# Input-projection weights requested on ScalarE's queue and a step later, stores of unit outputs a step later, next input rows a step sooner

## The chip, the cores and the metric

The program runs on one core of a Trainium2 chip. The metric is device time in microseconds (us) from one launch, shorter is better. Names used below: PE is TensorE (matmuls; PEld is its weight load), DVE is VectorE, ACT is ScalarE, POOL is GpSimd, SP is SyncE, which computes nothing and in this kernel only issues transfers (DMAs). ACT can issue DMAs too, between its own instructions and in their order.

## The reference

One encoder layer over two sequences (1024 and 2048 tokens of 1024 channels, all float32). The normed input goes through one wide projection; an FNet (Fourier) group and a bidirectional state-space group (24 heads of 64, in chunks of 128 tokens) work on its columns; both are gated, joined and projected back, then a gated per-layer embedding is added and a final norm taken.

```python
u = rms_norm(h, norm_w)
proj = u @ w_in
z_f, u_f, z_s, xbc, dt_raw = split(proj)
y_f = fft2(u_f).real @ w_fmix * silu(z_f)
xbc = silu(conv5(xbc) + conv_b)                 # -> xs, Bm, Cm
y_s = ssd(xs, dt_f, A_f, Bm, Cm) + flip(ssd(flip(...))) + D * xs
y_s = group_norm(y_s * silu(z_s)) * ssd_norm_w
h = h + concat(y_f, y_s) @ w_out
h = h + (p @ w_ple_in) * sigmoid(h @ w_ple_gate)
y = rms_norm(h, final_norm_w)
```

## The kernel before

Three phases follow each other: projection with the state-space group (to about 2085 us), the Fourier group (to about 2230 us), and the output projections with the end of the layer. The change touches the first alone. Its tokens come in three blocks of 1024: P (the short sequence), S1 and S2 (the halves of the long one).

**Steps.** In a block, 41 jobs each make 128 columns of the projection. A job has three pieces, one to a third of the block's tokens; a piece is 24 matmuls on a split of the float32 operands (`wh`, `wl` the weights' high and low part, `uh`, `ul` the tokens'), into one of three PSUM buffers `ps`. One piece is one step of a schedule that is written out by hand: `pre(s, f)` and `post(s, f)` put a function ahead of or behind the piece of step `s`, and every engine gets its instructions in that order. A block has 123 pieces. A state-space unit `u` (two heads; twelve to a block, one started every nine steps for most) is spread over some twenty steps by `Unit.plan`.

**Weights.** `Job.load` asks for the weights. In block P they come raw (`wr`, 512 KB); `Job.split` scales them on ACT (L327), makes `wh` (L333) there and `wl` on POOL (L334), and both are stored to memory (`WPd`). In S1 and S2 `load` fetches the stored `wh` and `wl` (512 KB each, L308), and `split` rounds them on ACT (L323). There are three buffers for `wh` and three for `wl`, so that a load waits for the last reader of the buffer that it takes.

**A unit's transfers.** `rows_in` asks for rows `R` (two of 256 KB at each of four steps, L551), which POOL cuts two steps later (`affine_select`, L559); ACT takes the exponent a step after that (L569), DVE joins them, PE uses them (`pd`, L586). POOL also makes `xw` (L598), which PE needs for the states (`pst`, L618). `decays` fetches `er` (eight requests of 64 partitions for a unit, L646). `gated` multiplies on POOL (L669; in S1 L674 too), and `out` stores `y` (L678) and, in S1, `zT` (L680).

**Next rows.** At a block's end `x_in` fetches nine tiles `xt` of the next block's tokens (L124), `x_norm` scales them on ACT (L225), and `x_turn` transposes them on PE (L239) into `uh` and `ul`.

**Queues.** Before the change all transfers of this phase are issued by SP, in order: an entry that has to wait holds all behind it. A finished transfer is told by one of eight semaphores (`DMAHW0` to `DMAHW7` in the listings of order), which are dealt out in turn over all transfers of the program; a transfer waits for the one that had its semaphore before to land. That is so for every issuing engine.

Of the kernel before, what the change touches and what calls it, by code (L numbers as in the profile page):

```python
# [9 lines left out]
F32 = mybir.dt.float32  # L10
# [8 lines left out]
P = 128  # L19
# [37 lines left out]
def tile_hybrid_encoder(ctx: ExitStack, tc: tile.TileContext, a):  # L57
    nc = tc.nc
# [45 lines left out]
    with ExitStack() as ph:  # L104
# [10 lines left out]
        def bank(shape, name):  # L115
            return bg.tile(shape, F32, tag="bg", name=name)
# [46 lines left out]
        w_in = a["w_in"][0]  # L163
# [46 lines left out]
        def flat(t):  # L210
            return t.rearrange("p k c -> p (k c)")
# [39 lines left out]
        before, behind_, slot = {}, {}, [0]  # L251

        def pre(s_, fn, *args):
            assert s_ >= slot[0], (s_, slot[0])
            before.setdefault(s_, []).append((fn, args))

        def post(s_, fn, *args):
            assert s_ >= slot[0], (s_, slot[0])
            behind_.setdefault(s_, []).append((fn, args))

        def step(piece=None):
            for fn, args in before.pop(slot[0], []):
                fn(*args)
            if piece is not None:
                piece()
            for fn, args in behind_.pop(slot[0], []):
                fn(*args)
            slot[0] += 1
# [18 lines left out]
        class Job:  # L287
# [16 lines left out]
            def load(self):  # L304
                if self.B.bi:
                    self.w = self.places()
                    for wt, kept in zip(self.w, self.kept):
                        nc.sync.dma_start(flat(wt).bitcast(F32), flat(kept))  # L308
                elif self.dt:
                    self.raw = sp.tile([P, KT, 64], F32, tag="R1", bufs=3, name="wdr")  # L310
                    V.memset(self.raw, 0.0)
                    for d in range(2):
                        nc.sync.dma_start(
                            self.raw[:, :, 32 * d:32 * d + 24],
                            w_in[:, C_DT + 24 * d:C_DT + 24 * (d + 1)].rearrange("(k p) c -> p k c", p=P))
                else:
                    self.raw = wp.tile([P, KT, P], F32, tag="wh", name="wr")
                    nc.sync.dma_start(self.raw, w_in[:, self.c0:self.c0 + P].rearrange("(k p) c -> p k c", p=P))

            def split(self):  # L320
                if self.B.bi:
# [214 lines left out]
        class Unit:  # L536
# [145 lines left out]
            def plan(self, s0):  # L682

                B, g = self.B, self.g
                self.y, self.xw, self.er, self.H, self.R, self.xm = {}, {}, {}, {}, {}, {}
                if self.u % 3 == 0:
                    for k, s_ in enumerate((1, 3) if g else (4, 5)):
                        post(s0 + s_, group_tokens, B, g, 4 * k)
                    for k, s_ in enumerate((6, 7)):
                        post(s0 + s_, group_cb, B, g, 4 * k)  # L690
                for p in range(4):
                    s_ = s0 + 4 + 2 * p
                    pre(s_, self.rows_in, p)
                    pre(s_ + 2, self.rows_cut, p)
                    pre(s_ + 3, self.rows_exp, p)
                    pre(s_ + 4, self.rows_joined, p)
                    post(s_ + 5, self.diag, p)
                post(s0 + 7, self.tokens, 0)
                pre(s0 + 8, self.weighted, 0, 0)
                post(s0 + 8, self.tokens, 4)  # L700
                pre(s0 + 6, self.state_in)
                pre(s0 + 9, self.weighted, 1, 4)
                post(s0 + 9, self.states, 0, 0)
                pre(s0 + 10, self.weighted, 0, 4)
                post(s0 + 10, self.states, 1, 4)
                pre(s0 + 11, self.weighted, 1, 0)
                post(s0 + 11, self.states, 0, 4)
                post(s0 + 12, self.states, 1, 0)
                for d in (1, 0):
                    pre(s0 + 11, self.decays, d, 0)  # L710
                    pre(s0 + 13, self.decays, d, 4)
                post(s0 + 14, self.across, 0)
                pre(s0 + 16, self.gated, 0)
                pre(s0 + 17, self.out, 0)
                post(s0 + 16, self.across, 4)
                pre(s0 + 18, self.gated, 4)
                pre(s0 + 19, self.out, 4)

        def norm_piece(b, i):

# [14 lines left out]
        def ple_weights():  # L735
            nc.sync.dma_start(PLd, a["w_ple_in"][0].rearrange("(k p) c -> p k c", p=P))
# [29 lines left out]
        n_, coming = 0, []  # L766
# [9 lines left out]
        for m in range(2, len(coming)):  # L776
            j = coming[m]
            if j.B.bi:
                pre(coming[m - 3].last + 1, j.load)
                pre(max(j.first - 2, coming[m - 3].last + 2), j.split)  # L780
            else:
                j.split_at = max(coming[m - 2].last + 1, coming[m - 1].split_at + 2)
                if m > 2:
                    pre(coming[m - 1].split_at + 1, j.load)
                pre(j.split_at, j.split)
# [3 lines left out]
        def x_in(b, i):  # L789
            xs[b["n"], i] = load_x(b, i)  # L790

        def x_norm(b, i):
            x_normed(b, i, xs[b["n"], i])

        def x_turn(b, i):
            x_turned(b, i, xs.pop((b["n"], i)))
# [5 lines left out]
        with tc.manual_schedule():  # L802
            b0 = BLOCKS[0]
            nc.sync.dma_start(nwr, a["norm_w"][0].rearrange("(t p) -> t p", p=P))
            x_in(b0, 0)
            x_in(b0, 1)
            x_in(b0, 2)
            coming[0].load()
            x_in(b0, 3)
            coming[1].load()  # L810
            x_in(b0, 4)
            pnw = bank([P, KT], "pnw")
            T.transpose(out=pnw, in_=nwr, identity=ident[:KT, :KT])
            V.tensor_copy(nwt, pnw)
            x_norm(b0, 0)
            x_norm(b0, 1)
            x_turn(b0, 0)
            x_norm(b0, 2)
            x_turn(b0, 1)
            coming[0].split()  # L820
            coming[2].load()
            x_in(b0, 5)
            x_norm(b0, 3)
            x_turn(b0, 2)
            coming[1].split()
            pre(0, small_in)
            post(2, small_constants)
            for i, (n_in, n_norm, n_turn) in enumerate(
                    ((0, 0, 0), (0, 0, 0), (0, 0, 1), (0, 1, 2), (1, 2, 2), (1, 2, 3)), 3):
                if i > 5:  # L830
                    pre(n_in, x_in, b0, i)
                if i > 3:
                    pre(n_norm, x_norm, b0, i)
                post(n_turn, x_turn, b0, i)
            pre(8, decay_rates)
            for (B, js, what), row in zip(rows_, pieces):
                bi, s0 = B.bi, slot[0]
                if what == "first":
                    q = s0 if bi else s0 + 1
                    post(q + 5, dt_turned, B)  # L840
                    pre(q + 6, dt_softplus, B, 0)
                    pre(q + 7, dt_softplus, B, 1)
                    post(q + 10, dt_sums, B)
                    post(q + 12, dt_rows, B)
                    pre(q + 14, dt_out, B)
                elif what == "last" and bi < 2:
                    b = BLOCKS[bi + 1]
                    for i, s_ in enumerate((3, 4, 5, 5, 6, 7, 7, 8, 9)):
                        pre(s0 + (0, 0, 1, 2, 3, 4, 5, 6, 7)[i], x_in, b, i)
                        pre(s0 + s_ - 1, x_norm, b, i)  # L850
                        post(s0 + s_, x_turn, b, i)
                elif isinstance(what, int):
                    B.units[what].plan(s0)
                    if 2 <= what < 10:
                        weight_sums(8 * bi + what - 2, s0)
                    if what == 3 and bi == 1:
                        ple_weights()
                    if what == 6 and bi < 2:
                        for i in range(9):
                            pre(s0 + 2 * i, norm_piece, BLOCKS[bi + 1], i)  # L860
                for j, si in row:
                    step(lambda: j.piece(si))
            while before or behind_:
                step()
# [315 lines left out]
    with ExitStack() as ph:  # L1180
# [85 lines left out]
        with tc.issue_after(ld.ins):  # L1266
            coming = prepare(0, 1)
# [4 lines left out]
        for n, (p, i) in enumerate(steps):  # L1272
            cur, after = ready, coming
            with tc.issue_after(ld.ins):
                if n + 2 < len(steps):
                    if steps[n + 2] == (1, 0):
                        incoming(1)
                    coming = prepare(*steps[n + 2])
# [136 lines left out]
```

## Time and profile before

| | |
|---|---|
| median of 3 runs | 3130.74 us (3124.7 to 3133.87) |
| profiled execution, its own time | 3149.84 us |
| span of its trace | 3148.0 us, granted TensorE clock 0.956 |
| busy in the span | PE 2868.9, DVE 2094.6, ACT 1590.6, POOL 1226.2 us |
| transfers | 525.56 MB, mean 167 GB/s; nearly all on SP's queue |

In the views, a name such as `wl<-WPd` says what is written from what, without buffer numbers. "SPq" or "ACTq" is an engine's issuing side. A row of a waiting view reads: who waited, for whom, us in total, times, longest. A row of a view by stretches reads: from and to, length, then for each engine the busy us and the number of instructions, the granted clock of PE, the share of the DMA engines' time that was busy, and GB/s. A row of a timeline reads: start, length, engine, line, operation, names, shapes, count, and in brackets the engine's idle time just before and what ended it; rows of equal instructions are merged.

### The profile page before, as it was taken

The page shows a single profiled execution, that of the slowest core. Times are in us where ns is not written, and L with a number is a line of the kernel's source. Part 1 is how long each engine was busy: PE and PEld are TensorE (multiplying, and loading weights), DVE is VectorE, ACT ScalarE, POOL GpSimd, SP SyncE. Part 2 cuts the span into 40 slices and gives each one's busy share as a digit, 9 for nine tenths or more (in the row PEclk, how much of TensorE's full clock was granted, in tenths as well). Part 3 has the DMA queues.
Part 4 walks back from the last instruction along what each step waited for, and adds up shares of the span by engine and source line. Part 5 has one row for each costly group of instructions (what it writes and reads, how often), then busy time and mean ns, then how long its engine had stood idle before and what let it go on. Part 6 is the DMA issues. An engine that isn't in the chain of part 4 may idle for free. (4 is left out here: it accounts for less than half of the span.)

```text
span 3148.0 us, 47800 instructions
## 1 busy us (share of the span) xinstructions
PE 2868.9 (91%) x17253; PEld 2599.0 (83%) x17253; DVE 2094.6 (67%) x3386; ACT 1590.6 (51%) x3417; POOL 1226.2 (39%) x1034
## 2 busy tenths in 40 slices
PE   6899889997999988997999999968999899989998
PEld 5898878886999888987999999967777677768887
DVE  1586756563676656655666675568889888866665
ACT  6556556554554455444655454434433443345554
POOL 0255444431143434341133243235687678720000
PEclk9999999998999999998999999988999999999999
DMA  3488887975587877774477777755654554452222
GB/s 113 144 177 204 196 213 196 205 186 164 131 178 191 188 204 181 187 178 140 137 174 171 186 182 172 171 153 213 219 178 150 207 168 154 138 202 91 83 78 78
DMA packets 406249, 525.56 MB, mean 167 GB/s; under 512 B 26984, under 2 KB 326132, under 8 KB 402172
## 3 DMA queue, kind: packets, MB, share of 16 engines
q1 hardware_dynamic: 405724, 521.45, 62.0%
q8 instruction: 137, 2.24, 0.3%
q14 instruction: 100, 0.82, 0.1%
q10 hardware_dynamic: 288, 1.05, 0.1%
HBM read 370.88 MB, written 152.57 MB: 166 GB/s over the span
## 5 line engine op out<-in xcount | busy, mean ns | idle before, releaser
L372 PE MATMUL ps<-uh,wh 128*128 128x342 f32 (+1 forms) x2880 | 967.8, 336 | 14.4 <-ACT uh L242 12.7
L372 PE MATMUL ps<-uh,wl 128*128 128x342 f32 (+1 forms) x2880 | 932.3, 324 | 1.8 <-POOL wl L334 1.8
L372 PE MATMUL ps<-ul,wh 128*128 128x342 f32 (+1 forms) x2880 | 932.5, 324 | 0.3 <-DVE ul L243 0.2
L372 PEld LDWEIGHTS ps<-uh,wh 128*128 128x128 f32 x2880 | 558.2, 194 | 27.2 <-ACT uh L242 13.5
L559 POOL TENSOR_SCALAR_AFFINE_SELECT R<-R 128x512 f32<-128x512 f32 x288 | 232.1, 812 | 857.5 <-DMA R<-ROWd 732.2
L372 PEld LDWEIGHTS ps<-ul,wh 128*128 128x128 f32 x2880 | 559.9, 194 | 1.7 <-DVE ul L243 1.2
L372 PEld LDWEIGHTS ps<-uh,wl 128*128 128x128 f32 x2880 | 555.7, 193 | 2.1 <-POOL wl L334 2.1
L569 ACT ACTIVATE R<-R,lb 128x128 f32<-128x128 f32 x1152 | 357.4, 391 | 188.3 <-POOL R L559 188.1
L334 POOL TENSOR_TENSOR wl<-wr,wh 128x1024 fp32r<-128x1024 f32 x40 | 98.5, 2464 | 351.8 <-ACT wh L333 337.1
L618 PE MATMUL pst<-xw,Bm 128*128 128x128 f32 x1056 | 160.9, 297 | 66.3 <-POOL xw L598 66.0
L629 DVE SCALAR_TENSOR_TENSOR H<-H,cd,pst 128x64 f32<-128x64 f32 x888 | 182.8, 275 | 49.4 <-PE pst L618 46.2
L618 PEld LDWEIGHTS pst<-xw,Bm 128*128 128x128 f32 x1056 | 141.1, 204 | 83.8 <-POOL xw L598 74.9
L1131 PE MATMUL X<-whP,ah 128*128 128x512 f32 x480 | 195.5, 407 | 6.3 <-ACT pu L1140 4.8
L1131 PE MATMUL X<-whP,al 128*128 128x512 f32 x480 | 192.8, 402 | 1.6 <-DVE al L1102 1.6
L1131 PE MATMUL X<-wlP,ah 128*128 128x512 f32 x480 | 193.4, 403 | 0.1
L598 POOL TENSOR_TENSOR xw<-xm,wd 128x512 f32<-128x512 f32 x144 | 175.2, 1222 | 46.0 <-PE pst L618 36.6
L413 DVE SCALAR_TENSOR_TENSOR xT<-raw,cvt,xT 128x1024 f32<-128x1024 f32 x144 | 189.8, 1318 | 2.6
L574 DVE TENSOR_TENSOR R<-R,R 128x512 f32<-128x512 f32 x144 | 133.9, 930 | 82.3 <-ACT R L569 29.1
L378 ACT COPY raw<-ps 128x342 f32<-128x342 f32 x180 | 77.6, 436 | 208.0 <-PE ps L372 207.9
L1243 POOL TENSOR_TENSOR ht<-ht,pu 128x512 f32<-128x512 f32 x96 | 156.2, 1635 | 63.6 <-ACT pu L1140 39.5
L1102 DVE TENSOR_TENSOR al<-s,ah 128x512 fp32r<-128x512 f32 x144 | 142.5, 1013 | 19.2 <-ACT ah L1101 19.1
L663 DVE TENSOR_TENSOR yt<-po,er 128x512 f32<-128x512 f32 (+1 forms) x144 | 91.2, 634 | 87.8 <-PE po L660 66.0
(272 smaller groups left out, 5850.9 us busy)
## 6 DMA issues: line engine op xcount, KB each, us to landing
R<-ROWd SPq DMA_DIRECT2D x288, 256.0 KB
wh<-WPd SPq DMA_DIRECT2D x80, 512.0 KB
wl<-WPd SPq DMA_DIRECT2D x80, 512.0 KB
er<-EXPd SPq DMA_DIRECT2D x288, 128.0 KB
Hd<-ht SPq DMA_DIRECT2D x48, 512.0 KB
ht<-Hd SPq DMA_DIRECT2D x48, 512.0 KB
y<-Yd SPq DMA_DIRECT2D x46, 512.0 KB
wlP<-WSd SPq DMA_DIRECT2D x21, 1024.0 KB
```

Of the source, the lines that this page charges most:

```text
L334: (V if self.dt else G).tensor_tensor(wl, raw, wh.bitcast(F32), op=ALU.subtract)
L372: T.matmul(ps[:, :n], lhsT=wt[:, kt, :], rhs=ut[:, kt, :n], start=(i == 0), stop=(i == 3 * KT - 1))
L413: V.scalar_tensor_tensor(dst, raw[:, k:k + TB], cvt[:, 20 * k + ct:20 * k + ct + 1], dst, op0=ALU.mult, op1=ALU.add)
L559: G.affine_select(out=R.rearrange("p c h l -> p (c h) l"), in_=R.rearrange("p c h l -> p (c h) l"), pattern=[[0, 4], [sgn, P]], compare_op ...
L569: S.activation(R[:, c, h, :], R[:, c, h, :], AF.Exp, bias=self.B.lb[:, 2 * p + c, hc + h:hc + h + 1])
L574: V.tensor_tensor(E[0], E[0], E[1], op=ALU.add)
L598: G.tensor_tensor(xw, self.xm[c4].rearrange("p c (h e) -> p c h e", h=2), col(self.B.wd[:, c4:c4 + 4, hc:hc + 2]).broadcast_to([P, 4, 2, 6 ...
L618: T.matmul(pst[:, c, :], lhsT=B.Bm[self.g][:, c4 + c, :], rhs=xw[:, c, :, :].rearrange("p h e -> p (h e)"), start=True, stop=True)
L629: V.scalar_tensor_tensor(dst[:, e], H[d][:, cc, e], B.cd[:, cc, hc + h:hc + h + 1], pst[:, c, e], op0=ALU.mult, op1=ALU.add)
L1102: V.tensor_tensor(al, src, ah.bitcast(F32), op=ALU.subtract)
L1131: T.matmul(ps, lhsT=at[:, k, :], rhs=wt[:, k, :], start=(first and i == 0), stop=(i == 11), skip_group_check=not first)
L1243: return lambda t: G.tensor_tensor(h, h, t, op=ALU.add)
```

## The change

Four edits. `Job.load` issues its transfers on ACT in S1 and S2, and in P from step 1 on. In S1 and S2 it stands at two steps behind the end of the job three back, instead of one; `split`, which came no sooner than two steps behind that job, comes no sooner than four behind it (for jobs that follow each other singly the other bound, two steps ahead of the job's first piece, already gave five). `out` stands two steps behind `gated` instead of one. Of the next block's nine tiles, six are asked for one step sooner.

```diff
                     for wt, kept in zip(self.w, self.kept):
-                        nc.sync.dma_start(flat(wt).bitcast(F32), flat(kept))
+                        nc.scalar.dma_start(flat(wt).bitcast(F32), flat(kept))
...
-                    nc.sync.dma_start(self.raw, w_in[:, self.c0:self.c0 + P].rearrange("(k p) c -> p k c", p=P))
+                    (nc.scalar if slot[0] else nc.sync).dma_start(self.raw, w_in[:, self.c0:self.c0 + P].rearrange("(k p) c -> p k c", p=P))
...
-                pre(s0 + 17, self.out, 0)
+                pre(s0 + 18, self.out, 0)
...
-                pre(s0 + 19, self.out, 4)
+                pre(s0 + 20, self.out, 4)
...
-                pre(coming[m - 3].last + 1, j.load)
-                pre(max(j.first - 2, coming[m - 3].last + 2), j.split)
+                pre(coming[m - 3].last + 2, j.load)
+                pre(max(j.first - 2, coming[m - 3].last + 4), j.split)
...
-                        pre(s0 + (0, 0, 1, 2, 3, 4, 5, 6, 7)[i], x_in, b, i)
+                        pre(s0 + (0, 0, 1, 1, 2, 3, 4, 5, 6)[i], x_in, b, i)
```

What each engine computes stays the same. 200 of the transfers of this phase leave SP's queue for ACT's: 38 of `wr`, 80 of `wh`, 80 of `wl` and 2 of the `dt` job's.

The first place is SP's queue in the middle of block P (`R` rows, `Yd` output store, `WSd` and `WPd` stores, `wb` another weight's load, `wr` the raw weights). Before:

```order
L318 DMA wr_3354<-in_w_in 128x8x128 [waits DMAHW7_49,Pool_49]
L678 DMA Yd0_60<-y_3113 128x512 [waits DMAHW0_49,Pool_49]
L551 DMA R0_3422<-ROWd0_67 128x2x256 [waits DMAHW1_49,PE_49]
L551 DMA R1_3424<-ROWd0_67 128x2x256 [waits DMAHW2_49]
L199 DMA WSd0_77<-wb_2953 128x2x256 [waits DMAHW3_49]
L200 DMA WSd0_77<-wb_2953 128x256 [waits DMAHW4_49]
L201 DMA WSd0_77<-ws_3208 128x4x256 [waits DMAHW5_49]
L263 DMA WPd25_0_130<-wh_3301 128x1024 [waits DMAHW6_49]
L263 DMA WPd25_1_131<-wl_3302 128x1024 [waits DMAHW7_49]
```

The same place on SP after the change:

```order
L551 DMA R0_3421<-ROWd0_67 128x2x256 [waits DVE_49,DMAHW7_49,PE_49,Pool_49]
L551 DMA R1_3423<-ROWd0_67 128x2x256 [waits DMAHW0_49,Activation_49,Pool_49]
L199 DMA WSd0_77<-wb_2953 128x2x256 [waits DMAHW2_49]
L200 DMA WSd0_77<-wb_2953 128x256 [waits DMAHW3_49]
L201 DMA WSd0_77<-ws_3208 128x4x256 [waits DMAHW4_49,Pool_49]
L263 DMA WPd25_0_130<-wh_3301 128x1024 [waits DMAHW5_49,Activation_49]
L263 DMA WPd25_1_131<-wl_3302 128x1024 [waits DMAHW6_49]
L678 DMA Yd0_60<-y_3113 128x512 [waits DMAHW7_49,Pool_49]
```

The load of `wr` has left the queue, and the rows `R` now stand ahead of the store of `y` instead of behind it.

The second place is SP's queue in the middle of block S1, where one unit's eight `er` stand. Before:

```order
L646 DMA er1_9600<-EXPd1_71 64x4x128 [waits DMAHW1_49]
L646 DMA er1_9600<-EXPd1_71 64x4x128 [waits DMAHW2_49]
L646 DMA er0_9603<-EXPd1_71 64x4x128 [waits DMAHW3_49]
L646 DMA er0_9603<-EXPd1_71 64x4x128 [waits DMAHW4_49]
L308 DMA wh_9652<-WPd24_0_128 128x1024 [waits DMAHW5_49,PE_49]
L308 DMA wl_9653<-WPd24_1_129 128x1024 [waits DMAHW6_49,PE_49]
L646 DMA er1_9719<-EXPd1_71 64x4x128 [waits DMAHW7_49]
```

And after the change, with the two stores that now stand ahead of them and one `er` more:

```order
L678 DMA Yd1_61<-y_9336 128x512 [waits DMAHW7_49,Pool_49]
L680 DMA ZSd_73<-zT_8637 128x512 [waits DMAHW0_49,Pool_49]
L646 DMA er1_9600<-EXPd1_71 64x4x128 [waits DMAHW1_49]
L646 DMA er1_9600<-EXPd1_71 64x4x128 [waits DMAHW2_49]
L646 DMA er0_9603<-EXPd1_71 64x4x128 [waits DMAHW3_49]
L646 DMA er0_9603<-EXPd1_71 64x4x128 [waits DMAHW4_49]
L646 DMA er1_9719<-EXPd1_71 64x4x128 [waits DMAHW5_49]
L646 DMA er1_9719<-EXPd1_71 64x4x128 [waits DMAHW6_49]
```

The two weight loads have left from between the `er`. A transfer signals with the semaphore that its row names, so that `DMAHW4` is now told by the last `er0_9603` and `DMAHW5` by the first `er1_9719`.

The third place is ACT at the same point of the program (`zT` a gate evicted from PSUM, `wh_9458` and `wh_9523` the same weights in the two builds, `R0` the exponents, `raw` an eviction). Before:

```order
L247 ACTIVATE zT_9665<-ps_9666 128x342 [waits DMAHW5_49,DMAHW1_49,PE_49]
L434 COPY Bm_9583<-ptt_9703 128x512 [waits PE_49]
L323 CAST wh_9458<-wh_9458 128x1024 [waits DMAHW0_49]
L323 CAST wl_9459<-wl_9459 128x1024 [waits DMAHW1_49]
L569 ACTIVATE R0_9537<-R0_9537,lb_8027 128x128 [waits DMAHW6_49,Pool_49]
```

After:

```order
L247 ACTIVATE zT_9661<-ps_9662 128x342 [waits DMAHW7_49,DMAHW0_49,PE_49]
L434 COPY Bm_9581<-ptt_9699 128x512 [waits PE_49]
L323 CAST wh_9523<-wh_9523 128x1024 [waits DMAHW2_49]
L323 CAST wl_9524<-wl_9524 128x1024 [waits DMAHW4_49]
L308 DMA wh_9707<-WPd24_0_128 128x1024 [waits DMAHW4_49]
L308 DMA wl_9708<-WPd24_1_129 128x1024 [waits DMAHW5_49]
L569 ACTIVATE R0_9535<-R0_9535,lb_8027 128x128 [waits DMAHW3_49,Pool_49]
```

Between the rounding of one job's weights and the exponents of a unit, ACT now issues the next job's loads, and each of them waits for one of the `er` transfers of the second place; no row of ACT's own work behind them starts before.

## The prediction

> **What bounds the kernel now.** I read the profile in this order: busy time by stretches cut at the blocks, what PE waited for in them, what SP's queue waited for, and two timelines. The stretches first (PE, PEld, DVE, ACT, POOL busy; then PE's granted clock, DMA share, GB/s):
>
> ```profile
> 100.00:700.00 600.00, 544.76 (x3691) 523.16 (x3690) 385.96 (x662) 359.63 (x905) 276.93 (x220) 0.96 0.81 192
> 700.00:790.00 90.00, 68.67 (x465) 63.91 (x462) 37.37 (x77) 40.80 (x84) 16.18 (x17) 0.87 0.62 168
> 790.00:1395.00 605.00, 567.00 (x3879) 547.50 (x3879) 380.72 (x704) 315.42 (x664) 226.17 (x225) 0.97 0.74 178
> 1395.00:1480.00 85.00, 64.33 (x425) 59.35 (x424) 36.10 (x75) 40.38 (x80) 23.62 (x23) 0.86 0.58 164
> 1480.00:2085.00 605.00, 586.52 (x4083) 566.62 (x4082) 393.62 (x756) 307.44 (x665) 183.85 (x198) 0.98 0.68 164
> 2085.00:3148.00 1063.00, 972.92 (x4368) 779.52 (x4368) 825.98 (x1051) 468.07 (x904) 488.25 (x342) 0.95 0.45 153
> ```
>
> The reader is to see that PE leads in all three blocks and what it leaves: 600 - 544.8 = 55.2 us idle in P, 605 - 567.0 = 38.0 in S1, 605 - 586.5 = 18.5 in S2, and 21.3 and 20.7 at the two boundaries. With the idle time comes a slower clock: 0.04 x 600 = 24 us in P, 0.03 x 605 = 18 in S1, 0.02 x 605 = 12 in S2, 0.13 x 90 = 12 and 0.14 x 85 = 12 at the boundaries. So a microsecond that PE stands costs some half a microsecond more (24/55, 18/38, 12/18.5, 24/42); I use 1.5 us for one. The last 1063 us are not touched.
>
> What PE waited for in P, S1 and S2 (three answers):
>
> ```profile
> PE pst L618 <- POOL xw L598: 41.9, 16, 5.5
> ...
> PE pst L618 <- POOL xw L598: 11.8, 6, 2.8
> PE pd L586 <- DVE R L575: 9.6, 2, 5.2
> PE pd L586 <- issue: 6.5, 1, 6.5
> ...
> PE pst L618 <- POOL xw L598: 11.3, 6, 2.7
> PE pd L586 <- ACT R L569: 2.7, 2, 2.2
> PE pd L586 <- DVE H L629: 2.1, 1, 2.1
> ```
>
> Nearly all of it is the chain of the rows `R`: POOL cuts rows in the same queue in which it makes `xw`, and it stands idle for them. Up to 2085 us, what POOL and ACT waited for, and SP's queue:
>
> ```profile
> POOL R L559 <- DMA R<-ROWd: 732.2, 162, 44.9
> POOL wl L334 <- ACT wh L333: 337.1, 38, 38.9
> ...
> ACT wr L327 <- DMA wr<-in_w_in: 69.8, 22, 7.9
> ...
> SPq L678 <- POOL y L669: 175.1, 42, 7.4
> SPq L308 <- PE ps L372: 134.3, 28, 12.1
> SPq L318 <- POOL wl L334: 127.1, 30, 18.7
> SPq L308 <- PE ps L364: 40.1, 2, 21.9
> ```
>
> SP stands 175 us at the store of `y`, 127 us at the load of raw weights and 174 us at the load of kept ones, with the next rows behind. One case, on SP:
>
> ```profile
> 329.21 0.37 SPq L318 DMA_DIRECT2D wr<-in_w_in  x1
> 336.08 0.33 SPq L678 DMA_DIRECT2D Yd<-y  x1
> 336.50 2.56 SPq L551 DMA_DIRECT2D R<-ROWd  x2
> ```
>
> From 329.6 to 336.1 SP is held at the store, 6.5 us, and the two rows go out behind it.
>
> **The change, part by part.** *Rows.* The stores a step later and the loads off the queue take these holds away. Rows are late for another reason too, their transfer: in the timelines of SP and ACT in S1,
>
> ```profile
> 952.73 4.09 SPq L646 DMA_DIRECT2D er<-EXPd  x4
> 956.92 1.21 SPq L308 DMA_DIRECT2D wh<-WPd  x1
> 958.23 2.63 SPq L308 DMA_DIRECT2D wl<-WPd  x1
> 961.68 8.60 SPq L646 DMA_DIRECT2D er<-EXPd  x4
> 970.39 2.04 SPq L551 DMA_DIRECT2D R<-ROWd  x2
> ...
> 959.79 1.28 ACT L569 ACTIVATE R<-R,lb 128x128 f32<-128x128 f32 x4
> ...
> 973.68 1.05 ACT L323 CAST wh<-wh 128x1024 fp32r<-128x1024 f32 x1 [0.34 <-DMA wh<-WPd]
> ...
> 981.78 1.28 ACT L569 ACTIVATE R<-R,lb 128x128 f32<-128x128 f32 x4 [5.58 <-POOL R L559]
> ```
>
> rows asked for at 970.39 are in use at 981.78, 11.4 us later, cut included. With a hold of 6.5 and a transfer of some 11 us, the part that goes is between none and all; I take half. P: 41.9 / 2 = 21 us; S1: (11.8 + 9.6 + 6.5) / 2 = 14; S2: (11.3 + 2.7 + 2.1) / 2 = 8; 43 us of standing, at 1.5 that is 64 us. Bounds: 0 and 129.
>
> *Next rows a step sooner.* Six of nine tiles are asked for earlier, but they wait for buffers as well, and PE's waits at the first boundary end at other work too:
>
> ```profile
> PE pt L239 <- DVE y L591: 8.6, 1, 8.6
> PE ps L364 <- ACT uh L242: 7.2, 2, 7.0
> ```
>
> I take 3 us a boundary, x 2 x 1.5 = 9 us; bounds: 0, and the 42 + 24 us that the boundaries lose.
>
> *Issuing on ACT.* 200 transfers go over. ACT issues two transfers late in the program already:
>
> ```profile
> L1074 ACTq DMA_DIRECT2D Yd<-yv x2: 327/332/337, 2226.2 to 2231.4; - x2
> ```
>
> At 0.33 us each they take 66 us of ACT over 1985 us, beside 240, 290 and 298 us that ACT is idle in P, S1 and S2 (stretches above). I take 0; without that cover it is 66.
>
> *ACT held at a load.* This is the new wait. A load now stands in ACT's order and waits for the transfer that had its semaphore. Behind it stand evictions of `ps` (three buffers), the exponents, and copies for `xw`: PE waits for these. In P the loads are where they were, about when ACT gets there, and ACT's 69.8 us for `wr` stand against the new holds: I take 0, with bounds of plus and minus 70. In S1 and S2 the third place of the listings is the worst, once a unit: the load waits for the first `er` of the group that SP issued from 961.68. Without the two L308 (1.21 and 2.63 us) that `er` goes out at some 957.9; if it takes 11 us as the rows do, it lands near 969, while ACT is there at 959.8: held 9 us. Can ACT lose 9 us? Its idle pieces from there to 981.8 include 5.58 us at the last row, and the evictions that PE needs are five microseconds apart:
>
> ```profile
> 950.89 0.44 ACT L378 COPY raw<-ps 128x342 f32<-128x342 f32 x1 [0.81 <-PE ps L372]
> ...
> 956.31 0.46 ACT L247 ACTIVATE zT<-ps 128x342 f32<-128x342 f32 x1 [3.70 <-PE ps L372]
> ```
>
> With three buffers PE may go on for about two pieces, 11 us, so a hold of 9 us is just borne, and one that is 4 us longer, or lands beside another, is not. Bounds: 0 and 9 us a unit, 24 units, 324 us. I take 4 us for half of S1's twelve units and 2 us for a quarter of S2's, which have no `ZSd` ahead of their `er`: (24 + 6) x 1.5 = 45 us lost.
>
> *The store of `zT` a step later.* In S1 ACT's next gate writes the same buffer. The store moves behind the rows of its step:
>
> ```profile
> 945.70 0.32 SPq L680 DMA_DIRECT2D ZSd<-zT  x1
> 948.01 2.48 SPq L551 DMA_DIRECT2D R<-ROWd  x2
> ```
>
> so from 945.7 to 950.5 or later, and the write at 956.31 has 4.8 us less. That is at most 4.8 us of ACT, 3.5 us of idle time ahead of the hold above, which it would shorten by as much: 0 beside it, 12 x 4.8 x 1.5 = 86 if it came on top.
>
> *Loads a step later.* The rounding stays five steps behind the old job, so the load has three steps instead of four. ACT's wait at 973.68 is 0.34 us, for a load issued at 956.92: there is no room at this place, but the weights are used two steps after. I take 0; it is up to 5 us of a step a unit, inside the bounds of the hold.
>
> **Sum.** 64 + 9 - 45 = 28 us gained. The sum is made against the profiled execution, 3149.84 us (span 3148.0 and 1.8 around it), which lies 19.1 above the median; I take it off the median: 3130.7 - 28 = 3103 us.
>
> **Rivals.** (1) *ACT becomes the bound*, the other side. One mechanism: the hold at the load behind the `er`, once a unit in S1 and S2. It costs 24 x 1.5 = 36 us for each microsecond of PE, so from 73 / 36 = 2 us a unit on the change loses. At 3 us: 108 - 73 = +35, 3166 us. For it: every third load there stands behind eight `er`, four of which keep SP 8.6 us in issuing alone; ACT's room is the two pieces. Against it: ACT is idle for half of S1 and S2, so that holds do not add up.
>
> (2) *All goes well:* three quarters of the row waits go and ACT is never held: 0.75 x 129 + 9 = 106, 3025 us. For it: 476 us of holds on SP against 86 us of waits on PE. Against: loads of the same bytes meet the same transfers.
>
> (3) *The rows come no sooner*, since the DMA engines are the limit: shares of 0.81, 0.74 and 0.68, and these are means. Then rows wait in the transfers for what SP no longer waits for, and with ACT's holds small it is 3131 us. The Trainium skill has a rule to this effect ("DMA: Bandwidth & Descriptors", section "Issuing engines are not separate DMA queues"): transfers of all issuing engines run on the same 16 DMA engines, and a second issuer saves only the time to initiate them. By it this case's gain is none unless initiating is what holds the rows. The trace speaks for the holds at the store, 6.5 us in one place, and for the rule in the stretch from 961.68, where four `er` take 8.6 us to issue and no engine is waited for.
>
> **How the numbers follow.** Forecast 0.43 (3103 us, by itself 3075 to 3128), rival 1 0.28 (3140 to 3200), rival 2 0.12 (3000 to 3060), rival 3 0.17 (3120 to 3142). About 0.3%, 9.4 us, is what a measurement of this kernel tells from no change: faster means under 3121, slower over 3140. Of the forecast 0.37 lies below 3121 and 0.06 within; rival 3 gives 0.03, 0.11 and 0.03; rival 1 0.01 within and 0.27 above; rival 2 0.12 below. Together 0.52, 0.18, 0.30. For eight in ten the range leaves out the better half of rival 2 (0.07) and the upper third of rival 1 (0.09), and most of the bounds' far ends with them: 3035 to 3180.
>
> **What would show it.** Right: in SP's waits the rows for L678 on POOL fall from 175 us to under 60 and L318 and L308 are gone; `pst` on `xw` falls from 41.9 to near 20 in P; ACT shows idle time that ends at `er` landings, under 10 us a unit. Wrong: PE's rows name `ps` or `xm` behind ACT, with more idle time in S1 or S2 than 38.0 and 18.5 us (rival 1), or POOL's 732 us for `R` and the DMA shares stay (rival 3).

## The result, and the profile after

The changed kernel takes 3238.29 us (median of 4 runs, 3223.02 to 3245.78) against 3132.30 us of the kernel before on the same chip (4 runs, 3124.7 to 3135.79): a ratio of 1.0336, 95% interval 1.0290 to 1.0381. It is slower by 106 us. The profiled execution took 3233.16 us, its span is 3231.0 us.

First the view by stretches, cut at the same matmuls as the stretches of before: P, its end, S1, its end, S2, the rest (PE, PEld, DVE, ACT, POOL busy; PE's clock, DMA share, GB/s).

```profile
100.90:804.60 703.70, 554.90 (x3691) 532.34 (x3690) 383.11 (x657) 352.82 (x894) 281.22 (x219) 0.88 0.69 164
804.60:891.60 87.00, 69.29 (x465) 65.43 (x462) 43.40 (x82) 45.38 (x93) 18.52 (x17) 0.88 0.51 163
891.60:1480.80 589.20, 557.07 (x3879) 537.48 (x3879) 379.20 (x703) 316.82 (x670) 247.82 (x231) 0.98 0.81 186
1480.80:1563.10 82.30, 63.87 (x425) 59.34 (x424) 37.14 (x76) 38.04 (x74) 19.56 (x18) 0.88 0.51 154
1563.10:2179.50 616.40, 586.75 (x4070) 565.73 (x4070) 394.77 (x755) 306.82 (x666) 188.94 (x198) 0.98 0.69 162
2179.50:3231.00 1051.50, 969.85 (x4382) 775.63 (x4381) 817.34 (x1052) 467.70 (x904) 492.68 (x342) 0.96 0.45 154
```

Nearly all of the loss is in one block. P took 600 us and takes 703.7; S1 went from 605 to 589.2, S2 from 605 to 616.4, and the untouched rest from 1063 to 1051.5, which tells how far two executions differ for no reason of the change. Against a second profile of the kernel before (before_again, further below: 588.5, 595.9 and 590.4 us) P lost 115 us and S2 26. In P, PE's idle time went from 55.2 to 703.7 - 554.9 = 148.8 us, its clock from 0.96 to 0.88, and the DMA share fell from 0.81 to 0.69: over the whole block the transfers are no nearer to their limit than before.

Now the groups of instructions in block P of the changed kernel (busy, mean ns of one, then the idle time just before and what ended it):

```profile
L327 ACT ACTIVATE wr<-wr,nwt 128x128 f32<-128x128 f32 x280 | 85.7, 390 | 224.9 <-DMA wr<-in_w_in 224.9
L422 DVE SCALAR_TENSOR_TENSOR xT<-raw,xT 128x1024 f32<-128x1024 f32 x11 | 27.7, 2520 | 146.9 <-ACT raw L421 146.9
L432 PE MATMUL ptt<-ident,xT 128*128 128x128 f32 x88 | 18.6, 350 | 139.3 <-DVE raw L345 63.7 <-DVE xT L422 47.7 <-DVE y L591 27.9
```

Read from below: 139.3 of PE's 148.8 idle us stand before one line, the transposes of a convolution's result. DVE had not finished it, because it waited 146.9 us for ACT's tanh (L421), and ACT stood 224.9 us at the scaling of raw weights, for their load. The row `ACT wr L327` read 69.8 us over all of the phase before. (A wait on DVE is put down to the instruction that came last there: L345, a filling of two columns, and L591 stand right behind L422.) One such place, first ACT and its issuing side:

```profile
361.20 0.37 ACTq L318 DMA_DIRECT2D wr<-in_w_in  x1
...
366.23 0.45 ACT L247 ACTIVATE zT<-ps 128x340 f32<-128x340 f32 x1 [1.76 <-PE ps L372]
381.17 2.44 ACT L327 ACTIVATE wr<-wr,nwt 128x128 f32<-128x128 f32 x8 [14.49 <-DMA wr<-in_w_in]
383.64 1.04 ACT L333 CAST wh<-wr 128x1024 fp32r<-128x1024 f32 x1
384.59 1.05 ACT L421 ACTIVATE raw<-xT 128x1024 f32<-128x1024 f32 x1
...
387.14 0.38 ACTq L318 DMA_DIRECT2D wr<-in_w_in  x1
```

DVE and PE behind it:

```profile
385.68 2.52 DVE L422 SCALAR_TENSOR_TENSOR xT<-raw,xT 128x1024 f32<-128x1024 f32 x1 [12.18 <-ACT raw L421]
...
388.34 1.09 PE L432 MATMUL ptt<-ident,xT 128*128 128x128 f32 x4 [10.70 <-DVE raw L345]
```

SP beside it:

```profile
357.98 1.03 SPq L551 DMA_DIRECT2D R<-ROWd  x2
360.45 1.14 SPq L263 DMA_DIRECT2D WPd<-wh  x1
363.44 1.06 SPq L263 DMA_DIRECT2D WPd<-wl  x1
365.39 7.75 SPq L551 DMA_DIRECT2D R<-ROWd  x4
```

And what the queues moved, in the 20 us of this load (361.2 to 381.2) and, below the dots, in the 4 us of the next one (387 to 391); q1 is SP's queue, q10 ACT's (packets, MB, share of the 16 engines' time):

```profile
q1 hardware_dynamic: 2078, 2.52, 81.8%
q10 hardware_dynamic: 1040, 0.52, 11.4%
...
q10 hardware_dynamic: 1040, 0.52, 48.1%
q8 instruction: 1, 0.02, 1.6%
q1 hardware_dynamic: 19, 0.02, 1.1%
```

A load of the same size takes 3.9 us when it is alone and 20 us when SP gives out rows and stores beside it; SP's entries came out around the load's request, since no raw load stands in SP's queue any more. In those 20 us the engines are 81.8 + 11.4 = 93% busy, by the time of their packets, and the load itself takes 11.4% of them, 2.3 us. The trace's packets show where its 20 us went: 6.2 us pass before its first packet (1.0 us for the load that is alone), and the last 90 of its 1040 packets take the last 6 us. The load has 504 B to a packet (0.52 MB / 1040: a packet of this view is a row of 512 B, 1024 of them, and 16 small ones), SP's transfers 1213 B (2.52 MB / 2078).

From this, **theory A**: in P one raw load at a time is in flight. A load waits for `wl` of the job before (L334 on POOL, which reads the buffer that it takes), that for `wh` (L333) and the scaling (L327) on ACT, and these for the load. The four parts of this chain, summed over 36 jobs from the times of issue, landing, start and end in the trace (the sums of all experiments, to which the text comes back; P is measured here from its first piece to the start of the last but one, a longer stretch than in the views):

```
us, 36 jobs of block P     issue to  landing  split to  wl to       sum   P, first to
                           landing   to split end of wl next issue        last but one piece
before, second profile       325       46      220         5        596   682
after                        420       57      217        23        717   809
p_loads_on_sp                315       62      220         3        599   683
only_p_loads                 376       64      216        71        727   813
own_buffer                   358      107      216       -21        661   752
big_pieces                   335       20      217        43        615   699
sp_big_pieces                307       51      221         1        580   662
own_buffer_alone             415       93      218      -125        602   678
sp_own_buffer                417      101      217      -140        595   670
```

The parts follow each other, so a sum is simply the time from one issue to the one 36 loads later; what tells of a chain is how little of it is slack (landing to split, and `wl` to issue). Before, that was some 50 of 596 us. After, the landings grew by 95 us and the sum by 121, and P by 127. In the chain of work that ended last, followed back through P, the raw load had 25.7% in the second profile of before (rows `R` 12.0%, `xw` 3.6%) and has 47.7% now: P hung on it in part before, and mostly on it after. What had to be found out: whether these loads are to blame alone, whether through the chain or through ACT's holds at its loads, and why a load beside SP's transfers is so slow.

### The profile page after: what moved, and what is told of

Same layout as the page of the kernel before. It is cut to its first block, busy times and chain, and to the rows that moved or that the text cites. A ratio compares the mean times of both kernels' runs of the same rounds, so it can differ in the third digit from the quotient of the medians.

```text
span 3231.0 us, 47693 instructions
## 1 busy us (share of the span) xinstructions
PE 2867.4 (89%) x17253; PEld 2595.8 (80%) x17253; DVE 2089.8 (65%) x3386; ACT 1586.6 (49%) x3417; POOL 1259.3 (39%) x1034
## 4 chain that ended last, share of the span: by engine, by line
DMA 42%; PE 28%; DVE 8%; ACT 8%; issue 6%; POOL 6%; SPq 1%; ACTq 0%; DVEq 0%; POOLq 0%
PE ps L372 11%; DMA wr<-in_w_in 10%; DMA wl<-WPd 8%; DMA er<-EXPd 7%; DMA R<-ROWd 5%; PE X L1131 5%; DMA xt<-in_x_sample 3%; PE Z L1131 3%; PE W L1321 2%; ACT wr L327 2%; DVE al L1102 2%; DMA wh<-WPd 2%; DVE s L1107 2%; POOL ht L1243 1%; POOL sq L898 1%
## 5 line engine op out<-in xcount | busy, mean ns | idle before, releaser
L559 POOL TENSOR_SCALAR_AFFINE_SELECT R<-R 128x512 f32<-128x512 f32 x288 | 245.2, 862 | 686.6 <-DMA R<-ROWd 541.7
L334 POOL TENSOR_TENSOR wl<-wr,wh 128x1024 fp32r<-128x1024 f32 x40 | 96.1, 2402 | 521.8 <-ACT wh L333 453.8
L598 POOL TENSOR_TENSOR xw<-xm,wd 128x512 f32<-128x512 f32 x144 | 182.6, 1273 | 88.9 <-PE pst L618 57.8
L327 ACT ACTIVATE wr<-wr,nwt 128x128 f32<-128x128 f32 x320 | 98.0, 390 | 241.7 <-DMA wr<-in_w_in 241.7
L248 DVE SCALAR_TENSOR_TENSOR zT<-zT,ps 128x342 f32<-128x342 f32 (+1 forms) x108 | 54.6, 506 | 228.6 <-ACT zT L247 228.3
L432 PE MATMUL ptt<-ident,xT 128*128 128x128 f32 x288 | 49.8, 301 | 162.2 <-DVE xT L422 68.8
L422 DVE SCALAR_TENSOR_TENSOR xT<-raw,xT 128x1024 f32<-128x1024 f32 x36 | 61.2, 1701 | 172.3 <-ACT raw L421 172.3
L432 PEld LDWEIGHTS ptt<-ident,xT 128*128 128x128 f32 x288 | 37.6, 154 | 166.4 <-issue 116.1
```

The costliest lines, as they stand in the source:

```text
L327: S.mul(raw[:, k], raw[:, k], nwt[:, k:k + 1])
L334: (V if self.dt else G).tensor_tensor(wl, raw, wh.bitcast(F32), op=ALU.subtract)
L432: T.transpose(out=pt[:, c, :], in_=src[:, (c4 + c) * P:(c4 + c + 1) * P], identity=ident)
L559: G.affine_select(out=R.rearrange("p c h l -> p (c h) l"), in_=R.rearrange("p c h l -> p (c h) l"), pattern=[[0, 4], [sgn, P]], compare_op ...
L598: G.tensor_tensor(xw, self.xm[c4].rearrange("p c (h e) -> p c h e", h=2), col(self.B.wd[:, c4:c4 + 4, hc:hc + 2]).broadcast_to([P, 4, 2, 6 ...
```

## Experiments

All kernels were run beside the kernel before on their chip; its medians were 3118.66, 3111.45 and 3112.38 us in the three groups. Ratios are against these.

### Which edit: raw loads back, and raw loads alone

```diff
 p_loads_on_sp, against the changed kernel
-(nc.scalar if slot[0] else nc.sync).dma_start(self.raw, ...)
+nc.sync.dma_start(self.raw, ...)
 only_p_loads, against the kernel before
-nc.sync.dma_start(self.raw, ...)
+(nc.scalar if slot[0] else nc.sync).dma_start(self.raw, ...)
```

> The changed kernel, but with block P's raw loads wr on SP's queue as before (S1's and S2's loads on ACT's queue a step later, stores a step later and rows a step sooner all stay). Theory A: in block P one raw load at a time is in flight, and load, split on ACT, wh, wl on POOL and the next load form one chain without a gap (607 us of it before, 717 after); on SP's queue the load went ahead of the rows and stores that SP held behind it, on ACT's queue it shares the DMA engines with them. Then P goes back to what it was and 3090 to 3130 us come out, the mean time from issue to landing of wr back to 9 to 10 us from 11.6. Rival B: P's loss comes from the stores a step later or the rows a step sooner, and not from the raw loads: 3200 us or more.

Measured: 3117.03 us, ratio 0.9989 (0.9972 to 1.0006).

> The kernel before with one edit alone: block P's raw loads wr on ACT's queue. Theory A (the chain of raw loads): nearly the whole loss comes back, 3200 to 3240 us, with wr at 11 us or more from issue to landing. Rival B (the loss comes from the other edits): 3115 to 3145 us.

Measured: 3257.60 us, ratio 1.0436 (1.0409 to 1.0464). The same rows as above, in block P, for it and then for the kernel with the loads back:

```profile
L327 ACT ACTIVATE wr<-wr,nwt 128x128 f32<-128x128 f32 x280 | 85.7, 390 | 192.9 <-DMA wr<-in_w_in 192.9
L432 PE MATMUL ptt<-ident,xT 128*128 128x128 f32 x88 | 18.6, 350 | 127.3 <-DVE raw L345 60.1 <-DVE xT L422 44.3 <-DVE y L591 22.8
```

```profile
L327 ACT ACTIVATE wr<-wr,nwt 128x128 f32<-128x128 f32 x288 | 88.1, 390 | 47.8 <-DMA wr<-in_w_in 47.8
L432 PE MATMUL ptt<-ident,xT 128*128 128x128 f32 x88 | 13.8, 281 | 4.9 <-ACT cb L533 3.6 <-DVE raw L345 1.3
```

Rival B falls: 38 transfers on another queue are the whole loss, and more than it (3257.6 us lies above the range that was given). In this kernel two parts of the chain grew by about as much: the landings by 51 us, to a mean of 10.4 (376 / 36), under the 11 that was expected, and the time from `wl` to the next issue by 66, which theory A had not named. There the load stands in ACT's order and waits, some 50 us in all, for transfers of SP that had its semaphore (a store of `wl` at eight loads, `er` at two). In the changed kernel this second part grew by 18 us only; beside the other edits the holds are shorter.

### The chain: a buffer of its own for the raw weights

```diff
 own_buffer, against the changed kernel
-self.raw = wp.tile([P, KT, P], F32, tag="wh", name="wr")
+self.raw = t4.tile([P, KT, P], F32, tag="t4", name="wr")
```

> The changed kernel with the raw weights wr in a buffer of the pool t4 (seven buffers that the convolutions use) and no longer in one of wh's three, so that the next raw load no longer waits for wl on POOL. Theory A: the chain of a job loses POOL's part (some 3 us of about 19.9 a job, 36 jobs), while each load still lands in 11 us or more beside SP's transfers: 3120 to 3175 us. Rival C: ACT is held at its loads by the semaphores of SP's transfers, and that is what costs P its time, not the chain: 3210 us or more, since the holds stay.

Measured: 3176.12 us, ratio 1.0171 (1.0143 to 1.0200). Half of the loss is gone with the wait for `wl`, while the loads stay on ACT: P falls by 57 us. That speaks for the chain and against rival C. The time lies just above what theory A allowed (3175 us): the loads that SP's transfers slow still land late (up to 24.9 us after their issue), and ACT then stands at the scaling, chain or no chain.

### Why the load is slow: rows of 4 KB, on either queue

```diff
 big_pieces (against the changed kernel) and sp_big_pieces (against p_loads_on_sp), behind step 0
-w_in[:, self.c0:self.c0 + P].rearrange("(k p) c -> p k c", p=P)
+w_in[P * (self.c0 // P % 8):P * (self.c0 // P % 8 + 1), 0:KT * P].rearrange("p (k c) -> p k c", c=P)
```

> The changed kernel, with block P's raw loads on ACT's queue taken from other places of w_in: as many bytes (512 KB), but in rows of 4 KB, where the 128 columns of a job are rows of 512 B. The projection is then made with other weights. Theory A1: beside SP's transfers a queue gets its share of the DMA engines by packets, so that packets of 512 B get little: with 4 KB the mean of wr falls from 11.6 to 8 us or less, and 3130 to 3180 us come out. Theory A2: the share goes by bytes or by time of the engines, and the size of packets does not matter: wr stays at 11 us or more, 3215 to 3250 us.

Measured: 3124.06 us, ratio 1.0013 (0.9995 to 1.0031). Block P's rows:

```profile
L327 ACT ACTIVATE wr<-wr,nwt 128x128 f32<-128x128 f32 x283 | 86.8, 390 | 109.4 <-DMA wr<-in_w_in 109.4
L432 PE MATMUL ptt<-ident,xT 128*128 128x128 f32 x88 | 17.0, 327 | 44.7 <-DVE raw L345 24.2 <-DVE xT L422 15.0 <-DVE y L591 5.6
```

> The changed kernel with block P's raw loads on SP's queue, and taken from other places of w_in in rows of 4 KB instead of 512 B (the projection is made with other weights): the other half of the comparison that big_pieces began. Theory A1: the size of the packets matters only beside another queue; in one queue the load still lands after 7.5 to 9.5 us (8.7 with 512 B) and the time is 3100 to 3125 us. Rival G: rows of 4 KB are simply fetched faster, whatever stands beside them: wr lands after 6 us or less, and the time falls under 3095 us.

Measured: 3092.84 us, ratio 0.9934 (0.9906 to 0.9962).

On ACT's queue the size of the rows decides most of it. There, 4 KB in place of 512 B for as many bytes takes the ratio from 1.0336 to 1.0013, 3.2 points; on SP's queue from 0.9989 to 0.9934, 0.55 points. So the queue costs 1.0336 - 0.9989 = 3.5 points with rows of 512 B, and 0.8 with rows of 4 KB. Theory A2 falls. A1's numbers were off: the landing went from 11.7 to 9.3 us (335 / 36), not under 8, and the time fell below A1's range (3130 to 3180). What went is the spread, by the 36 issues and landings in each trace: a quarter took over 17.5 us in the changed kernel and over 11.0 with 4 KB rows (the longest 23.0 and 15.3). Split by the load's packets, the mean time to the first packet stayed (3.7 and 3.5 us), and the time from there to the landing fell from 8.0 to 5.8 us. A slow load stops ACT, and a fast one, early, gives nothing back. On SP the landing stayed as A1 said (8.7 and 8.5 us), so that rival G's reason falls, though the time, under 3095 us, is the one that G gave and lies below A1's. Those 17 us lie in P (683 to 662 us); where they come from is not settled. The 4 KB rows also come from eight places, each read some five times; on SP that left the landing as it was, on ACT's queue it was not tested apart.

The Trainium skill has an account that fits in part ("DMA: Bandwidth & Descriptors", section "Queues, rings and completion order"): each DMA engine takes turns between the queues that have work for it, a packet at a time. With turns of that kind a queue of small packets gets few bytes. The runs agree in their times, as far as those from the first packet to the landing go. The counts of the profile (504 B beside 1213 B) don't decide it: a packet in them is a row, and the page has several descriptors to a packet. No run here shows how many rows one turn takes, and the wait for the first packet is not explained by it.

### The other edits, one at a time

```diff
 only_stores, only_rows, only_kept_loads: the lines of the change for out; for x_in;
 for the kept loads (L308 on ACT, load and split later); each against the kernel before
```

> The kernel before with one edit alone: the stores of unit outputs a step later. The other edits without block P's raw loads gave 0.9989 together and the kept loads alone 1.0009, so that stores and rows together are worth some 0.2%. Theory H: SP no longer stands at the store of y (175 us of its waits) and the rows R come sooner, but PE is not bound by them: within 0.3% of before, 3100 to 3120 us. Rival I: the rows were what PE waited for, and the time falls by the 64 us that the prediction gave them or by a good part of it: under 3095 us.

Measured: 3112.28 us, ratio 0.9996 (0.9977 to 1.0015). SP's waits up to 2100 us in this kernel, and then the first three in the second profile of before:

```profile
SPq L308 <- PE ps L372: 155.1, 29, 12.1
SPq L318 <- POOL wl L334: 148.4, 35, 18.7
SPq L308 <- DMA R<-ROWd: 58.9, 30, 4.3
...
SPq L678 <- POOL y L669: 17.6, 7, 5.0
```

```profile
SPq L678 <- POOL y L669: 183.4, 47, 8.5
SPq L308 <- PE ps L372: 130.4, 27, 12.1
SPq L318 <- POOL wl L334: 125.8, 33, 18.7
```

The hold at the store fell by 166 us, and nothing came of it: SP waits at the loads instead, and PE's wait for `xw` is 62.5 us in this kernel and 47.9 in that profile. Rival I falls.

> The kernel before with one edit alone: six of the next block's nine tiles asked for a step sooner. Theory H: the two boundaries lose less (27 and 25 us before for two pieces each, 21 and 16 with three edits), worth up to 15 us: 3095 to 3112 us. Rival J: the boundaries are shortened by the stores or the kept loads, and this edit alone does nothing or costs: 3109 to 3125 us.

Measured: 3108.98 us, ratio 0.9981 (0.9962 to 1.0000): perhaps 6 us. The boundaries, where it was expected, are not shorter (30 and 26 us for two pieces each, 27 and 25 in the second profile of before), so the time lies in theory H's range but not for H's reason, and the interval reaches 1: whether this edit gains anything alone is open.

> The kernel before with one edit alone: S1's and S2's loads of wh and wl on ACT's queue, two steps behind the job three back, their rounding no sooner than four behind it. Theory D: with SP free of these loads the rows come sooner, and the holds of ACT at its loads stay inside what PE can bear: 3095 to 3113 us. Rival E: holds and rows cancel in this edit already, or the holds cost more: 3115 to 3150 us, with ACT idle for er by 100 us or more.

Measured: 3115.73 us, ratio 1.0009 (0.9993 to 1.0024); ACT stands 132.6 us for `er`. Rival E, at its near end: in the traces S1 is 15 us shorter and S2 12 longer than in the second profile of before, and each boundary 4 longer.

> The kernel before, unchanged, for a second profile of it beside those of this chip: 3115 to 3130 us, with block P some 8 us shorter than in the first profile, whose execution lay 19 us above its median.

Measured: 3109.53 us in a single run, below what was expected; P is 11.5 us shorter than in the first profile. Its stretches P, S1 and S2:

```profile
99.60:688.10 588.50, 543.40 (x3691) 522.09 (x3690) 387.32 (x662) 359.53 (x905) 276.78 (x220) 0.96 0.80 195
...
778.10:1374.00 595.90, 563.82 (x3880) 544.01 (x3879) 382.30 (x704) 315.12 (x664) 226.88 (x225) 0.97 0.77 181
...
1456.90:2047.30 590.40, 579.97 (x4074) 560.52 (x4073) 390.68 (x754) 306.62 (x665) 182.38 (x198) 0.99 0.71 167
```

### A version that is faster than both

> The changed kernel with block P's raw loads wr back on SP's queue and in a buffer of the pool t4, so that a load no longer waits for wl on POOL. Theory A: with the loads on SP, too, P is held by its chain of raw loads (599 us of about 593 that P takes, PE busy 550.5 of them); without POOL's part (2.4 us or more a job, 36 jobs) the chain is some 510 us and PE is the bound: of P's 43 us of idle PE half or more goes, 3065 to 3100 us. Rival F: the hold of SP at the raw load was what kept the rows and stores behind the load; without it the transfers meet and the load lands later by what it is asked for sooner: 3105 to 3130 us.

Measured: 3099.46 us, ratio 0.9961 (0.9942 to 0.9980), at the upper end of theory A's range. But the landings became as slow as in the changed kernel (417 us), and PE's idle time from P's first piece to its last but one fell only from 58 to 52 us, not by half.

> The kernel before with one thing changed: block P's raw loads wr, on SP's queue, in a buffer of the pool t4, so that a load no longer waits for wl on POOL. Theory A: P was held by its chain of raw loads, and shortens by the 12 us that the same step gave beside the other edits (682 to 670 us) or more: 3080 to 3102 us. Rival K: what was gained there came from the other edits' earlier rows and stores: 3105 to 3125 us.

Measured: 3105.64 us, ratio 0.9982 (0.9960 to 1.0005). Its only edit is the line of `own_buffer`, made to the kernel before. That is rival K's range, not theory A's: P shortened by 4 us and not by 12, so that taking the wait for `wl` out of the chain is worth next to nothing by itself.

> The same, and the next block's rows a step sooner: the candidate for a version faster than both kernels. If both gains add up, 3075 to 3100 us; if the rows bring nothing, the time of the one before.

Measured: 3097.24 us, ratio 0.9940 (0.9915 to 0.9965): faster than both kernels, by the buffer and the rows together; either alone can't be told from no change. The chain sums say why the buffer brings so little on SP's queue. The load is asked for some 3.5 us sooner (125 / 36) and takes 2.5 us longer ((415 - 325) / 36): in one queue it stands behind rows and stores and lands hardly sooner. That is rival F, in part: in sp_own_buffer P still shortened from 683 to 670 us.

## Why the prediction was wrong

**What bounds the kernel** failed first. The prediction read P as PE's block with waits for `xw` in it. A row that hinted at another limit was in its own fence, `POOL wl L334 <- ACT wh L333: 337.1, 38`: nearly one wait for each of 40 raw loads, each of which waits for the one before. In the second profile the chain had 46 + 5 = 51 us of slack in 596, about as little as PE's 45 us of idle time in P. That the chain alone set P's length before is not shown: without its wait for `wl` (own_buffer_alone) P shortened by 4 us.

**ACT held at a load** is the step that failed, in P: "the loads are where they were, about when ACT gets there", taken as 0, bounds plus and minus 70. The loss lies outside these bounds. The loads were asked for at the same event, but not in the same company. On SP the load stood ahead of the rows and stores behind it in the queue; on ACT it shares the engines with them, lands later (11.7 us in the mean, up to 23.0, where it was 9.0), and ACT stands at the scaling for it, 224.9 us of P against 49.3 in the second profile. Measured: 136 us for this edit alone (0.0436 of 3118.7), and 109 us on top of the other three (1.0336 - 0.9989 = 0.0347, of 3132.3). The diff and the listing showed the queue; what was not costed was the load's landing, which the prediction took from a trace in which the load had its place in line.

**Rows.** The mechanism was half right. With all four edits SP's wait at the store is 70.4 us (forecast under 60) and those at L318 and L308 are gone; `pst` no longer waits for `xw` in P or S1, and in S2 for 1.0 us. In P the wait for `xw` went because PE stands elsewhere. With the raw loads back on SP, SP's wait at the store is 57.6 us, and PE's wait for `xw` in P is what it was (second profile of before, then p_loads_on_sp):

```profile
L618 PE MATMUL pst<-xw,Bm 128*128 128x128 f32 x308 | 51.2, 313 | 33.4 <-POOL xw L598 33.3
...
L618 PE MATMUL pst<-xw,Bm 128*128 128x128 f32 x308 | 51.5, 314 | 34.7 <-POOL xw L598 34.6
```

So SP's hold at the store was not what made `xw` late in P, and the 64 us did not follow: without the raw loads on ACT the three other edits give 0.9989, where PE's idle time in P is 591.4 - 548.9 = 42.5 us, against 588.5 - 543.4 = 45.1 in the second profile of before. In S1 the wait for `xw` does go (9.0 us in the second profile), but PE's idle time there falls only from 32.1 to 28.5 us. What makes `xw` late in P stays open.

**S1 and S2: holds at the load.** ACT's waits for `er`, first in S1, then in S2:

```profile
ACT R L569 <- DMA er<-EXPd: 33.3, 7, 6.9
...
ACT R L569 <- DMA er<-EXPd: 66.2, 11, 12.5
...
ACT wl L323 <- DMA wl<-WPd: 38.4, 18, 9.1
```

That is 2.8 and 5.5 us a unit (twelve units each): the hold exists, under 10 us a unit as forecast (the longest single one is 12.5), but it is heavier in S2, which the step took to be the lighter one. PE's idle time in S1 is 589.2 - 557.1 = 32.1 us, just as in the second profile (595.9 - 563.8); in S2 29.6 against 10.4 there and 18.5 in the first. So, net of what earlier rows gave, S1 paid nothing of the 24 us of standing set aside for it, and S2 some 11 to 19 instead of 6. The kept loads alone, with what they free on SP, come to 1.0009, about 3 us; what the holds cost by themselves was not separated.

**The small terms.** Issuing on ACT at 0 stands: no row of ACT names it. The store of `zT` a step later does hold ACT in S1 (19.3 us, 5 times), and PE's idle time there did not rise: 0 was right. The next rows' 9 us are near the 6 measured, which can't be told from none and did not come at the boundaries. Loads a step later: ACT now waits 38.4 us for `wl` in S2, which may be part of the loss there.

**Rivals.** Rival 1 had the sign and the engine, ACT held at a load, but the wrong block, and the wrong price: not the semaphore's hold in S1 and S2, but a load in P that lands late. Rival 3 and its rule that issuers share the same DMA engines point the right way: the second issuer gained nothing. Yet by them the time would have stayed at 3131 us; the second issuer also took away the place of the raw load ahead of other transfers.

## What to carry to other kernels

Before a transfer moves to another queue, ask what it stood ahead of: a wait that holds a queue also keeps the later entries out of the way of the one that waits. Look for the loop in which a load waits for the use of the load before, and ask how much of it is slack over the block; if that is little, added landing time comes out as block time (here 95 us of landings, 121 us of the loop, 127 us of P), and the waits of the busiest engine may only be where it shows. A load in short rows goes into a queue where it has few others beside it, and a wait that vanishes from a list (166 us here) is worth nothing until the engine at the end moves.

## What the runs showed of the hardware that was not expected

- A load of 512 KB in rows of 512 B took 3.9 us alone and 20 us beside 2.5 MB of another queue, while it took 2.3 us of the engines' time; the longest was 23.0 us, and 15.3 us with rows of 4 KB. The time to the first packet was the same with both rows (3.7 and 3.5 us in the mean).
- The price of the second queue was 3.5% with rows of 512 B and 0.8% with rows of 4 KB; in one queue the same change of rows was worth 0.55%.
- PE's granted clock fell to 0.88 in P, where it stood 148.8 of 703.7 us, and was 0.96 where it stood 45.1 of 588.5.
